# Mixture-of-experts kernel: an expert's transposes move into the next expert's first block, third products into the gate bank

## The chip, the cores and the metric

The kernel runs on one core of a Trainium2 chip. The metric is the device time of one execution in microseconds (us), as the median of several runs; lower is better. Beside it stands one execution taken with the hardware profiler, whose span (first to last instruction) is a little shorter than its device time.

## The reference, cut to what matters

The reference is two layers of a sequence mixer, a second hybrid mixer, and then a mixture of 16 experts over 256 tokens, of which each token takes two. The change touches only the last part:

```python
def _hier_moe(h, rg_w, rg_b, re_w, re_b, w_gate, w_up, w_down):
    hf = h.reshape(bsz * s, d)                       # 256 tokens x 1024
    ...                                              # combine: 256 x 16 weights, two per token not zero
    out = jnp.zeros((bsz * s, d), jnp.float32)
    for e in range(N_EXPERTS):                       # 16
        act = jax.nn.silu(hf @ w_gate[e]) * (hf @ w_up[e])                  # 256 x 512
        out = out + combine[:, e:e + 1] * (act @ w_down[e]).astype(jnp.float32)
    return out.astype(h.dtype).reshape(bsz, s, d)
```

All of it is float32.

## The kernel before, in words

The mixers fill the first 440 us. Then `experts` (L1934) takes the 16 experts in turn, four to a group (`q, j = divmod(e, 4)`). Weights come over one DMA queue (SyncE) in chunks of 2 MB, three per expert (two for gate and up, one for down), into a ring of seven buffers; `give_back` lets a buffer be filled again once the products that read it are done. All instructions of an engine run in the order in which the Python code writes them down (`manual_schedule`), so a step's place in the loop is its place in the queue of every engine that it uses.

For a group, `gather_all` picks the tokens of its four experts into `xg` with matmuls. An expert's tokens lie in slots: 32 in a first block, 32 in a second, 32 in a third. Numbers of tokens are read from memory on the chip, and `tc.If` runs the second block only above 32 tokens and the third only above 64. In this trace experts 0, 2, 4, 6, 8, 10 and 12 have a second block, 4 and 8 a third one as well, and 1, 3, 5, 7, 9, 11, 13, 14 and 15 the first alone (seen from the matmuls that ran). An `If` that is not taken still leaves a mark on its engines, which later instructions wait for as they would for the work itself.

The steps of an expert e, each with its engines:

- `gate_up(e)` (L1728, PE): the products with the gate and up weights. The first block goes to the PSUM bank `gu`, the other two to two banks of the pair `mbank("s")`; the bank holds gate and up, each as two partial sums (even steps in rows 0:64, odd ones in 64:128). `product32` (L1708) is eight steps k of two matmuls for a block, which show as 32 in the trace.
- `down(e - 1)` (L1799, PE): the product of the expert before with its down weights, into the bank `dn`.
- `activate(e)` (L1758, ScalarE and VectorE by turns): adds the partial sums, takes silu, multiplies, and leaves the result in `sg`; the second and third block within an `If`.
- `turn(e)` (L1784): four PE transposes of `sg` into an `mbank("s")` (L1789), copied by ScalarE to `aT` (L1791).
- `take(e - 1)` (L1806): copies the product in `dn` to `y`. Above 32 tokens that is a ScalarE copy (L1815) and a VectorE copy (L1816); else a ScalarE copy to `t3` (L1820) and two VectorE adds (L1797).
- `third(e - 1)` (L1825, PE) and `take_third(e - 1)` (L1834): the down product of a third block, in a bank of its own, and its copies to `y2` (L1837, L1797); without a third block a one-column matmul (`none`, L1726) and nothing.

After every second expert `split_all` or `split_third` (L1849, L1850) scales `y` and cuts it into a high and a low part on ScalarE and VectorE, and `scatter_all` (L1679, eight matmuls) adds the rows to the four accumulators. `spread` (L1636, L1637) transposes the pick matrix of a group for the scatters; its copies go over ScalarE. The order in the loop of before, on PE: `gate_up(e)`; for some e a scatter or a spread; `down(e - 1)`; `turn(e)`; `third(e - 1)`; for j = 1 the scatter of third blocks, for j = 3 the scatter of the first two experts and the next gather. ScalarE and VectorE run `activate(e)`, the copy of `turn(e)`, `take(e - 1)`, `take_third(e - 1)`, then the splits.

Of the kernel before, what the change touches and what calls it, by code (L numbers as in the profile page):

```python
# [19 lines left out]
NT, KT = T // P, D // P  # L20
# [10 lines left out]
N_EXP = 16  # L31
R1, R2 = 4, 5
WARM = (18, 12, 3, 4, 2)
# [213 lines left out]
class Net:  # L247
# [1457 lines left out]
        nc.gpsimd.memset(self.y[0], 0.0)  # L1705
        nc.gpsimd.memset(self.y2, 0.0)

    def product32(self, out, w, n, lhs):  # L1708


        for k in range(n):
            for i in range(2):
                r = 64 * (k % 2) + 32 * i
                self.nc.tensor.matmul(out[r:r + 32, :], lhs(k), w(k)[:, HALF * i:HALF * i + HALF], start=(k < 2),  # L1714
                                      stop=(k >= n - 2), tile_position=(0, r))
# [9 lines left out]

        self.nc.tensor.matmul(b[:, 0:1], self.zero, w.bitcast(BF16)[:, 1:2], start=True, stop=True)  # L1726

    def gate_up(self, e):  # L1728

        j, tc = e % 4, self.tc  # L1730
        ws, rs = zip(*[self.load() for _ in range(2)])
        ws = [a.rearrange("p (k n) -> p k n", k=4) for a in ws]

        def w(k):
            return ws[k // 4][:, k % 4, :]

        def x(s):
            return lambda k: self.S["xg"][:, k, s:s + 32]
        banks = self.gus = [self.gu, self.mbank("s"), self.mbank("s")]

        def none(i):
            for a in ws[2 - i:]:
                self.none(banks[i], a[:, 0, 0:1])
        if e + 1 < N_EXP:
            self.count(e + 1)
        self.product32(banks[0], w, KT, x(64 * j))
        with tc.If(self.n[e] > 32) as more:
            self.product32(banks[1], w, KT, x(64 * j + 32))
            with tc.If(self.n[e] > 64) as much:
                self.product32(banks[2], w, KT, x(256 + 32 * j))  # L1750
            with much.Else():
                none(2)
        with more.Else():
            none(1)
            none(2)
        self.give_back(*rs)
# [67 lines left out]

    def third(self, e, aT, wd):  # L1825

        b = self.mbank("s")
        with self.tc.If(self.n[e] > 64) as more:
            self.product32(b, lambda k: wd[:, k, :], 4, lambda k: aT[:, k, 64:96])
        with more.Else():  # L1830
            self.none(b, wd[:, 0, 0:1])
        return b
# [101 lines left out]
    def experts(self):  # L1934
        nc, m = self.nc, self.mw
        self.acc = [[self.ps.tile([P, HALF], F32, name=f"acc{t}{h}") for h in range(2)] for t in range(NT)]
        self.gu, self.dn = (self.ps.tile([P, HALF], F32, name=n) for n in ("gu", "dn"))
        self.clear(self.gu)
        self.clear(self.dn)
        for a in self.acc:  # L1940
            for b in a:
                self.open(b)
        self.sg = m.tile([P, HALF], F32, name="sg")
        nc.gpsimd.memset(self.sg, 0.0)
        S = self.S = {}
        self.wq = {}
        NQ = N_EXP // 4

        def gather_all():
            S["xg"] = m.tile([P, KT, 384], F32, name="xg")  # L1950
            for k in range(KT):
                self.gather(self.oh, S["xg"], k)
                if k == KT - 1:
                    self.wq[len(self.wq)] = self.weights(len(self.wq), self.oh)
        gather_all()
        self.residual()
        self.n, self.na = {}, {}
        self.count(0)
        aT = oT = None
        wd = lambda w: w.rearrange("p (k n) -> p k n", k=4)  # L1960
        E = mybir.EngineType
        nq = naq = None
        for e in range(N_EXP):
            q, j = divmod(e, 4)
            more, last = q + 1 < NQ, e == N_EXP - 1
            if last:
                w, r = self.load()
                self.down(e - 1, aT, wd(w))
                self.take(e - 1)
                self.scatter_all(oT[:, 0, :])  # L1970
                self.split_all(slice(0, 64), self.wq[q][:, 1:2])
            self.gate_up(e)
            if j == 0 and q:
                c = self.cnt[0:1, 16 + q:17 + q]
                nq = nc.values_load(c, engines=(E.PE,), min_val=0, max_val=T)
                naq = nc.values_load(c, engines=(E.Activation, E.DVE), min_val=0, max_val=T)
            if j == 1 and q:
                self.scatter_all(oT[:, 1, :])
            if j == 2 and q:
                oT = self.spread(self.oh)  # L1980
            if e and not last:
                w, r = self.load()
                self.down(e - 1, aT, wd(w))
            self.activate(e)
            if e == 0:
                oT = self.spread(self.oh)
            if last:
                self.tc.mark_branch_hint_location("further", "LikelyTaken")
                for _ in range(WARM[3]):
                    self.clear(self.dn)  # L1990
            a0, aT = aT, self.turn(e)
            if e and not last:
                self.take(e - 1)
                b = self.third(e - 1, a0, wd(w))
                self.give_back(r)
                self.take_third(e - 1, b, self.na[e - 1])
            if j == 1 and q:
                with self.tc.If(naq > 64):
                    self.split_third(q - 1, self.y[1:])
                with self.tc.If(nq > 64) as much:  # L2000
                    self.scatter_all(oT[:, 2, :])
                with much.Else():
                    for h in range(2):
                        for y in self.y[1:]:
                            self.nc.tensor.matmul(self.acc[1][h][:, 0:1], self.zero,
                                                  y.bitcast(BF16)[:, h * D + 1:h * D + 2], start=False, stop=False)
            if j == 2:
                if more:
                    self.oh = self.picks(q + 1)
                self.split_all(slice(0, P), self.wq[q][:, 0:1])  # L2010
            if j == 0 and q:
                self.split_all(slice(0, P), self.wq[q - 1][:, 1:2])
            if j == 3 and more:
                self.scatter_all(oT[:, 0, :])
                gather_all()
        i = self.free.pop()
        self.last = self.rings[i].tile([P, 4096], F32, name=f"wchunk{i}")
        for i in range(2):
            self.row(4 + i, self.last[:, i * D:(i + 1) * D], eng=nc.sync)
        free = list(self.free)[:4]  # L2020
        left = [(e - 1, a0, wd(w))]
        w, r = self.load()
        left.append((e, aT, wd(w)))
        for _ in range(WARM[4]):
            self.clear(self.dn)
        self.down(N_EXP - 1, aT, wd(w))
        self.take(N_EXP - 1, True)
        self.further(free, left, oT)
        self.scatter_all(oT[:, 1, :], last=True)
# [65 lines left out]
```

## Time and profile before

| what | value |
|---|---|
| median of 3 runs | 708.78 us (708.65 to 710.01) |
| the profiled execution's own time | 709.35 us |
| its span | 707.6 us |
| busy: PE, VectorE, ScalarE | 630.5, 445.2, 314.5 us |
| granted TensorE clock, mean of the span | 0.952 of full speed |

The profiled execution is 0.57 us above the median, and 1.75 us of it lie outside the span. The rows below give, of a timeline, the start in us from the start of the span, the length, engine, line, operation and tiles; in brackets stands how long the engine had been idle and what ended that. An engine named with a q (DVEq) is the engine's sequencer, which runs branches and marks. The granted clock is 1.00 at 2.4 GHz and 0.50 at 1.2 GHz.

### The profile page before, as it was taken

To read this page: it belongs to the slowest core of one execution; us is meant where nothing else is said; L and a number is where in the kernel's file an instruction comes from. 1 tells how busy PE (TensorE), PEld (TensorE's weight loads), DVE (VectorE), ACT (ScalarE), POOL (GpSimd) and SP (SyncE) were. 2 spreads that over 40 slices of the span, in tenths; PEclk is the share of its full clock that TensorE was granted. 3 is DMA by queue.
4 is the path that set the end of the run, shared out by engine and by line. 5 is a ranking of instruction groups with operands and counts; after the bars stand their busy time and mean duration, and the time that the engine had idled before them with its cause. 6 is when DMAs were issued, how large, how long until landed. Compare 5 with 4: busy or idle time off the path is not lost. (4 is left out here: it accounts for less than half of the span.)

```text
span 707.6 us, 11743 instructions
## 1 busy us (share of the span) xinstructions
PE 630.5 (89%) x4487; PEld 445.7 (63%) x4487; DVE 445.2 (63%) x1050; ACT 314.5 (44%) x618; POOL 7.2 (1%) x29
## 2 busy tenths in 40 slices
PE   7999999899899999999999979899786978797771
PEld 4789888688897887898888866326222623262221
DVE  5898677878986786886778867443314332434235
ACT  5764554557455544435545425333314232434230
POOL 1000000000000000000000000100000000000001
PEclk9999999999999999999989998999999989899786
DMA  8956313243560034735033389999999879889011
GB/s 319 424 172 240 120 82 119 90 177 133 223 230 13 5 120 181 322 138 204 35 119 120 120 338 396 389 422 426 427 425 427 380 320 396 359 356 353 7 63 61
DMA packets 15917, 163.65 MB, mean 231 GB/s; under 512 B 1888, under 2 KB 2144, under 8 KB 6624
## 3 DMA queue, kind: packets, MB, share of 16 engines
q1 hardware_dynamic: 15552, 161.84, 57.3%
q8 instruction: 48, 0.79, 0.4%
q10 hardware_dynamic: 288, 0.79, 0.3%
q14 instruction: 29, 0.24, 0.1%
HBM read 161.57 MB, written 1.05 MB: 230 GB/s over the span
## 5 line engine op out<-in xcount | busy, mean ns | idle before, releaser
L318 ACT ACTIVATE whi<-wchunk 128x1024 fp32r<-128x1024 f32 (+2 forms) x103 | 107.4, 1043 | 94.3 <-PE pj L420 49.1
L319 DVE TENSOR_TENSOR wlo<-wchunk,whi 128x1024 fp32r<-128x1024 f32 (+2 forms) x103 | 123.1, 1198 | 18.7 <-ACT whi L318 18.4
L419 PE MATMUL pj<-xh,whi 128*128 128x256 f32 (+1 forms) x440 | 126.8, 289 | 0.0
L420 PE MATMUL pj<-xl,whi 128*128 128x256 f32 (+1 forms) x440 | 126.3, 287 | 0.0
L421 PE MATMUL pj<-xh,wlo 128*128 128x256 f32 (+1 forms) x440 | 125.3, 285 | 0.0
L419 PEld LDWEIGHTS pj<-xh,whi 128*128 128x128 f32 (+1 forms) x440 | 82.6, 188 | 3.2 <-issue 2.2
L420 PEld LDWEIGHTS pj<-xl,whi 128*128 128x128 f32 (+1 forms) x440 | 82.7, 188 | 2.8 <-issue 1.9
L421 PEld LDWEIGHTS pj<-xh,wlo 128*128 128x128 f32 (+1 forms) x440 | 82.6, 188 | 1.8 <-issue 1.6
L1714 PE MATMUL gu<-wchunk,xg 128*32 128x512 f32 x512 | 69.6, 692 | 4.5 <-issue 3.5
L1767 DVE TENSOR_TENSOR tg<-tg,gu 64x256 f32<-64x256 f32 x32 | 13.2, 413 | 71.5 <-ACT tg L1766 71.4
L1714 PEld LDWEIGHTS gu<-wchunk,xg 128*32 128x32 f32 x512 | 17.8, 125 | 44.7 <-issue 43.5
L420 PE MATMUL pj<-wlo,xh 128*128 128x512 f32 (+2 forms) x112 | 40.4, 360 | 1.6 <-DVE wlo L319 1.6
L419 PE MATMUL pj<-whi,mh 128*128 128x512 f32 x96 | 38.4, 403 | 2.6 <-ACT mh L510 2.1
L420 PE MATMUL pj<-wlo,mh 128*128 128x512 f32 x96 | 38.1, 398 | 2.5 <-DVE wlo L319 2.5
L419 PE MATMUL pj<-whi,xh 128*128 128x512 f32 (+2 forms) x112 | 39.0, 354 | 1.1 <-ACT whi L318 1.1
L421 PE MATMUL pj<-whi,xl 128*128 128x512 f32 (+2 forms) x112 | 39.9, 356 | 0.0
L421 PE MATMUL pj<-whi,ml 128*128 128x512 f32 x96 | 37.5, 399 | 0.0
L1766 ACT ACTIVATE tg<-gu 64x256 f32<-64x256 f32 x32 | 12.2, 381 | 51.4 <-PE gu L1714 32.7
L553 ACT ACTIVATE prob<-bank,smst 128x128 f32<-128x128 f32 (+1 forms) x64 | 26.1, 419 | 18.4 <-DVE smst L551 18.4
L1679 PE MATMUL acc<-y,oT 128*128 128x512 f32 x80 | 25.0, 454 | 8.5 <-ACT y L1849 7.3
L1714 PE MATMUL mbs<-wchunk,xg 128*32 128x512 f32 x288 | 32.3, 592 | 0.0
L1789 PE MATMUL mbs<-cstm,sg 96*128 96x96 f32 x64 | 9.6, 278 | 20.0 <-DVEq L1774 9.4
(414 smaller groups left out, 1068.8 us busy)
## 6 DMA issues: line engine op xcount, KB each, us to landing
wchunk<-wstream SPq DMA_DIRECT2D x67, 2048.0 KB, 11.3
wchunk<-wstream SPq DMA_DIRECT2D x12, 512.0 KB, 10.7
wchunk<-wstream SPq DMA_DIRECT2D x2, 1536.0 KB, 9.7
wchunk<-wstream SPq DMA_DIRECT2D x2, 1024.0 KB, 8.4
wchunk<-wstream SPq DMA_DIRECT2D x4, 436.0 KB, 5.6
wchunk<-wstream SPq DMA_DIRECT2D x1, 1744.0 KB, 6.7
wchunk<-xt SPq DMA_DIRECT2D x4, 256.0 KB, 5.4
X<-x SPq DMA_DIRECT2D x4, 256.0 KB, 5.9
```

Source lines behind the costliest of these rows:

```text
L318: nc.scalar.activation(hi, w, AF.Copy)
L319: nc.vector.tensor_sub(lo, w, hi.bitcast(F32))
L419: mm(out, ah, bh, start=start, stop=False)
L420: mm(out, ah, bl, start=False, stop=False)
L421: mm(out, al, bh, start=False, stop=stop)
L553: nc.scalar.activation(p[:, e, j, :N], S[e][:, j, :], AF.Exp, bias=nm[:, e, j:j + 1], accum_out=sm[:, e, j:j + 1])
L1679: self.nc.tensor.matmul(self.acc[t][h], oT[r, t * P:(t + 1) * P], y[1 + i], start=False, stop=last and i == 1, **at)
L1714: self.nc.tensor.matmul(out[r:r + 32, :], lhs(k), w(k)[:, HALF * i:HALF * i + HALF], start=(k < 2), stop=(k >= n - 2), tile_position=(0, r))
L1766: nc.scalar.activation(tg[0:64, 0, s], b[64:128, s], AF.Copy)
L1767: V.tensor_add(tg[0:64, 0, s], tg[0:64, 0, s], b[0:64, s])
L1789: nc.tensor.transpose(ps[:, n * i:n * i + n], self.sg[p, P * i:P * i + P], self.ident[p, p])
```

## The change

`turn(e - 1)` is no longer called after `activate(e - 1)`. `gate_up(e)` gets it as `mid` and runs it ahead of the last two of the eight steps k of its first block; it asks for its two `mbank("s")` only after that. `take(e - 1)` thereby stands before the copy of `turn(e)` in the queues of ScalarE and VectorE. `third` writes to `self.gu` in place of a bank of its own. The scatter of third blocks moves from the end of an expert with j = 1 to after the gate and up products of the next one, ahead of `spread`; the scatter with `oT[:, 0, :]` moves from the end of j = 3 to after its gate and up products. The first `spread` comes before `activate(0)`. For the last expert, `turn(14)` and the scatter come first, then `down(14)`, and `turn(15)` stands after the loop.

```diff
--- before.py
+++ after.py
@@ -1705,10 +1705,12 @@
         nc.gpsimd.memset(self.y[0], 0.0)
         nc.gpsimd.memset(self.y2, 0.0)
 
-    def product32(self, out, w, n, lhs):
+    def product32(self, out, w, n, lhs, mid=None):
 
 
         for k in range(n):
+            if k == n - 2 and mid:
+                mid()
             for i in range(2):
                 r = 64 * (k % 2) + 32 * i
                 self.nc.tensor.matmul(out[r:r + 32, :], lhs(k), w(k)[:, HALF * i:HALF * i + HALF], start=(k < 2),
@@ -1725,7 +1727,7 @@
 
         self.nc.tensor.matmul(b[:, 0:1], self.zero, w.bitcast(BF16)[:, 1:2], start=True, stop=True)
 
-    def gate_up(self, e):
+    def gate_up(self, e, mid=None):
 
         j, tc = e % 4, self.tc
         ws, rs = zip(*[self.load() for _ in range(2)])
@@ -1736,14 +1738,19 @@
 
         def x(s):
             return lambda k: self.S["xg"][:, k, s:s + 32]
-        banks = self.gus = [self.gu, self.mbank("s"), self.mbank("s")]
+        banks = self.gus = [self.gu]
+
+        def before():
+            if mid:
+                mid()
+            banks.extend(self.mbank("s") for _ in range(2))
 
         def none(i):
             for a in ws[2 - i:]:
                 self.none(banks[i], a[:, 0, 0:1])
         if e + 1 < N_EXP:
             self.count(e + 1)
-        self.product32(banks[0], w, KT, x(64 * j))
+        self.product32(banks[0], w, KT, x(64 * j), before)
         with tc.If(self.n[e] > 32) as more:
             self.product32(banks[1], w, KT, x(64 * j + 32))
             with tc.If(self.n[e] > 64) as much:
@@ -1824,7 +1831,7 @@
 
     def third(self, e, aT, wd):
 
-        b = self.mbank("s")
+        b = self.gu
         with self.tc.If(self.n[e] > 64) as more:
             self.product32(b, lambda k: wd[:, k, :], 4, lambda k: aT[:, k, 64:96])
         with more.Else():
@@ -1964,12 +1971,18 @@
             q, j = divmod(e, 4)
             more, last = q + 1 < NQ, e == N_EXP - 1
             if last:
+                aT = self.turn(e - 1)
+                self.scatter_all(oT[:, 0, :])
                 w, r = self.load()
                 self.down(e - 1, aT, wd(w))
                 self.take(e - 1)
-                self.scatter_all(oT[:, 0, :])
                 self.split_all(slice(0, 64), self.wq[q][:, 1:2])
-            self.gate_up(e)
+                self.gate_up(e)
+            else:
+                def mid():
+                    nonlocal aT
+                    aT = self.turn(e - 1)
+                self.gate_up(e, mid if e else None)
             if j == 0 and q:
                 c = self.cnt[0:1, 16 + q:17 + q]
                 nq = nc.values_load(c, engines=(E.PE,), min_val=0, max_val=T)
@@ -1977,26 +1990,6 @@
             if j == 1 and q:
                 self.scatter_all(oT[:, 1, :])
             if j == 2 and q:
-                oT = self.spread(self.oh)
-            if e and not last:
-                w, r = self.load()
-                self.down(e - 1, aT, wd(w))
-            self.activate(e)
-            if e == 0:
-                oT = self.spread(self.oh)
-            if last:
-                self.tc.mark_branch_hint_location("further", "LikelyTaken")
-                for _ in range(WARM[3]):
-                    self.clear(self.dn)
-            a0, aT = aT, self.turn(e)
-            if e and not last:
-                self.take(e - 1)
-                b = self.third(e - 1, a0, wd(w))
-                self.give_back(r)
-                self.take_third(e - 1, b, self.na[e - 1])
-            if j == 1 and q:
-                with self.tc.If(naq > 64):
-                    self.split_third(q - 1, self.y[1:])
                 with self.tc.If(nq > 64) as much:
                     self.scatter_all(oT[:, 2, :])
                 with much.Else():
@@ -2004,6 +1997,23 @@
                         for y in self.y[1:]:
                             self.nc.tensor.matmul(self.acc[1][h][:, 0:1], self.zero,
                                                   y.bitcast(BF16)[:, h * D + 1:h * D + 2], start=False, stop=False)
+                oT = self.spread(self.oh)
+            if e == 0:
+                oT = self.spread(self.oh)
+            if j == 3 and more:
+                self.scatter_all(oT[:, 0, :])
+            if e and not last:
+                w, r = self.load()
+                self.down(e - 1, aT, wd(w))
+            self.activate(e)
+            if e and not last:
+                self.take(e - 1)
+                b = self.third(e - 1, aT, wd(w))
+                self.give_back(r)
+                self.take_third(e - 1, b, self.na[e - 1])
+            if j == 1 and q:
+                with self.tc.If(naq > 64):
+                    self.split_third(q - 1, self.y[1:])
             if j == 2:
                 if more:
                     self.oh = self.picks(q + 1)
@@ -2011,16 +2021,19 @@
             if j == 0 and q:
                 self.split_all(slice(0, P), self.wq[q - 1][:, 1:2])
             if j == 3 and more:
-                self.scatter_all(oT[:, 0, :])
                 gather_all()
+        self.tc.mark_branch_hint_location("further", "LikelyTaken")
+        for _ in range(WARM[3]):
+            self.clear(self.dn)
+        a0, aT = aT, self.turn(N_EXP - 1)
         i = self.free.pop()
         self.last = self.rings[i].tile([P, 4096], F32, name=f"wchunk{i}")
         for i in range(2):
             self.row(4 + i, self.last[:, i * D:(i + 1) * D], eng=nc.sync)
         free = list(self.free)[:4]
-        left = [(e - 1, a0, wd(w))]
+        left = [(N_EXP - 2, a0, wd(w))]
         w, r = self.load()
-        left.append((e, aT, wd(w)))
+        left.append((N_EXP - 1, aT, wd(w)))
         for _ in range(WARM[4]):
             self.clear(self.dn)
         self.down(N_EXP - 1, aT, wd(w))
```

## Rows read from the trace of the kernel before

**Rows 1.** Windows: busy time of PE, PEld, DVE, ACT, POOL, then PEclk, DMA share, GB/s.
```profile
450.00:500.00 50.00, 46.38 (x351) 21.01 (x355) 17.17 (x36) 16.75 (x34) 0.00 (x0) 0.97 1.00 420
...
600.00:650.00 50.00, 43.09 (x301) 19.87 (x293) 19.71 (x39) 18.36 (x36) 0.00 (x0) 0.93 0.87 347
```

**Rows 2.** Waits of the DMA queue from 420 us on: total us, times, longest.
```profile
SPq L292 <- PE mbs L1726: 128.2, 20, 15.2
```

**Rows 3.** Groups of instructions by line from 440 us on: busy, mean ns, idle before.
```profile
L1797 DVE TENSOR_TENSOR y<-tg,dn 32x512 f32<-32x512 f32 x18 | 12.2, 680 | 22.3 <-ACTq L1836 13.9 <-ACT tg L1820 8.1
...
L1789 PE MATMUL mbs<-cstm,sg 96*128 96x96 f32 x64 | 9.6, 278 | 20.0 <-DVEq L1774 9.4 <-DVE sg L1770 8.0 <-DVEq L1772 2.6
...
L1820 ACT ACTIVATE tg<-dn 64x512 f32<-64x512 f32 x9 | 5.3, 592 | 6.5 <-PE dn L1714 6.4
...
L1816 DVE COPY y<-dn 64x512 f32<-64x512 f32 x7 | 4.8, 692 | 24.0 <-ACTq L1836 14.8 <-ACT y L1815 9.2
...
L1815 ACT ACTIVATE y<-dn 64x512 f32<-64x512 f32 x7 | 4.0, 578 | 0.0
```

**Rows 4.** Line 1836, the branch of take_third: its marks, and who waited for it.
```profile
L1836 DVEq EVENT_SEMAPHORE  x12: 21/21/21, 463.7 to 670.6; - x12
...
  PEld dn L1714: 2.8, 1
```

**Rows 5.** Timeline of PE around the last expert.
```profile
667.44 0.52 PE L1789 MATMUL mbs<-cstm,sg 96*128 96x96 f32 x4 [0.83 <-DVEq L1772]
...
670.64 3.32 PE L1714 MATMUL dn<-wchunk,aT 128*32 128x512 f32 x16 [2.67 <-ACT y L1849]
673.89 2.12 PE L1679 MATMUL acc<-y,oT 128*128 128x512 f32 x8
675.93 3.64 PE L1714 MATMUL gu<-wchunk,xg 128*32 128x512 f32 x32
```

**Rows 6.** Timeline of PE after experts 2 (first row) and 4.
```profile
471.99 0.52 PE L1789 MATMUL mbs<-cstm,sg 96*128 96x96 f32 x4 [1.10 <-DVEq L1774]
...
505.72 0.52 PE L1789 MATMUL mbs<-cstm,sg 96*128 96x96 f32 x4 [3.98 <-DVE sg L1770]
...
506.91 4.98 PE L1714 MATMUL gu<-wchunk,xg 128*32 128x512 f32 x32 [0.57 <-issue]
```

**Rows 7.** Timeline of PE after expert 1.
```profile
457.75 3.65 PE L1721 MATMUL dn<-wchunk,aT 128*64 128x512 f32 x16
...
461.83 3.64 PE L1714 MATMUL gu<-wchunk,xg 128*32 128x512 f32 x32
```

**Rows 8.** Timeline of PE after expert 13.
```profile
646.85 3.65 PE L1721 MATMUL dn<-wchunk,aT 128*64 128x512 f32 x16
...
653.72 4.14 PE L1679 MATMUL acc<-y,oT 128*128 128x512 f32 x8 [2.73 <-ACT y L1849]
657.80 4.63 PE L1714 MATMUL gu<-wchunk,xg 128*32 128x512 f32 x32
```

**Rows 9.** Timeline of PE after experts 5 (first two rows) and 9.
```profile
518.00 1.92 PE L1714 MATMUL mbs<-wchunk,aT 128*32 128x512 f32 x16
...
522.91 5.34 PE L1714 MATMUL gu<-wchunk,xg 128*32 128x512 f32 x32 [0.47 <-issue]
...
592.63 0.49 PE L1679 MATMUL acc<-y,oT 128*128 128x512 f32 x1 [2.38 <-ACT y L1849]
...
595.23 3.64 PE L1714 MATMUL gu<-wchunk,xg 128*32 128x512 f32 x32
```

**Rows 10.** Timeline of PE after expert 0.
```profile
451.80 0.69 PE L1636 MATMUL dn<-cstm,oh 128*128 128x128 f32 x2 [2.46 <-ACT oT L1637]
...
453.06 4.60 PE L1714 MATMUL gu<-wchunk,xg 128*32 128x512 f32 x32
```

**Rows 11.** Windows of one us after two idle stretches; columns as in rows 1.
```profile
507.00:508.00 1.00, 1.00 (x8) 0.31 (x12) 0.58 (x1) 0.38 (x1) 0.00 (x0) 0.50 1.08 459
...
593.00:594.00 1.00, 0.71 (x4) 0.49 (x4) 1.00 (x2) 0.27 (x1) 0.00 (x0) 1.00 1.00 426
```

## The prediction

> **What bounds the kernel now.** I first asked the windows who is short of what in the expert part. PE is busy 46.4 of 50 us at 450 to 500 and 43.1 at 600 to 650, while the DMA share falls from 1.00 to 0.87 [rows 1]. The DMA queue's own waits say why: it stands 128.2 us in 20 waits for PE to hand buffers back [rows 2]. So the weights are ahead, and PE's sequence with its waits sets the end. What PE waits for stands in the groups: the transposes (L1789) are busy 9.6 us and are preceded by 20.0 us of idle PE, ended by VectorE's activation [rows 3]. The timeline shows the pattern: after expert 4 PE idles 3.98 us, transposes in 0.52 us, and starts the next first block 1.19 us after the transposes began, at 506.91 [rows 6]. Idle PE costs twice: that block takes 4.98 us in place of 3.64 [rows 6, 7], since the granted clock stands at 0.50, the 1.2 GHz level, after the idle stretch [rows 11].
>
> **The idea and what it meets.** The change puts products ahead of the transposes: `down`, and three quarters of the next first block. If nothing else held that block, the 20.0 us would mostly go. But `third` now writes the gate bank, and `take_third` reads it, so the next first block may start only when ScalarE and VectorE have gone past the branch of `take_third(e - 1)`. They get there after `activate(e)` and `take(e - 1)`, which stand ahead of it in their queues. That the branch is mostly not taken doesn't help: it leaves 12 marks, and PE waited 2.8 us for one of them, that of expert 13, which has no third block [rows 4]. There VectorE's mark came at 670.6 and PE's `down` began at 670.64 [rows 4, 5]. So the block that was to cover the activation waits for the activation and for the copies too.
>
> The Trainium skill bears on this (PSUM — Partial Sum Buffer, section "PSUM bank collisions raise a hardware error"): two engines must not touch one bank and quadrant at once, and accesses are to be ordered by bank, not address. By that rule the wait is needed and the time is my sum; without it, it is the first rival's.
>
> **The turn from one expert to the next, part by part.** S is the start of the transposes now, G that of the next first block.
>
> *Even experts 2 to 12 (six turns).* At S the activation is done. What follows on VectorE is two adds of 0.680 us [rows 3]; the ScalarE copy ahead of them, 0.592 us [rows 3], runs beside the last activation product. Two branches lie on the way; no row gives their whole price. The mark itself is 21 ns [rows 4]; I take 0.2 us each, with ends 0 and 0.4. New G is S + 1.36 + 0.4 = S + 1.8, against S + 1.19 [rows 6]: 0.6 later. Then the block holds the transposes, 0.52 [rows 6], without a wait of their own. 1.1 slower each, 6.6 in all.
>
> *Extra in turns 6 and 10.* A scatter now goes before `spread`, and ScalarE's copies of `spread` go before `activate`, so the activation starts later by all of it. After 10 that is eight matmuls, 2.12 us [rows 5]: +2.0. After 6 it is four one-column matmuls and a branch: +0.5, estimated.
>
> *Turn 1.* `down(0)` ends at 457.75 + 3.65 = 461.40. Its two copies run one after the other, 0.578 and 0.692 [rows 3], with about 0.35 for semaphores and branches: new G is 463.0 against 461.83 [rows 7]. With the transposes +1.7.
>
> *Turn 13.* The same copies after 646.85 + 3.65 = 650.50 give 652.15 against 657.80, where the wait for the split of third blocks (2.73) and a slow scatter (4.14) went before [rows 8]. That is -5.65, the transposes +0.5, and the block of 4.63 us returns to 3.64: -1.0. Together -6.1.
>
> *Turns 5 and 9.* The third block of 4 and 8 is there, so its copy is awaited in earnest. After 5 the product ends at 519.92, now 0.5 earlier without the transposes; copy, adds and branch take 0.6 + 1.4 + 0.4: G is 521.8 against 522.91 [rows 9], with the transposes in the block -0.6. After 9 the product ended at 592.63 - 2.38 = 590.25; the same gives 592.1 against 595.23 [rows 9], with the transposes -2.6.
>
> *Turn 0.* PE idles 2.46 us in `spread`, since ScalarE copies it behind the activation, and the next block takes 4.60 [rows 10]. With `spread` ahead, the activation starts later by its copies and the transposes inside the block wait about 1.2: +0.5.
>
> *Turns 3, 7, 11.* The gather lies between, longer than the copies: only the order changes, 0.
>
> *The end.* After 14 the scatter of 2.12 delays S from 667.44 to 669.5. The copies take 1.8, the first split another 0.8, so the scatter for 12 and 13 runs from 672.0; its last quarter waits for the second split, to 674.2. `down(14)` at full clock is half of its 3.32 and a little, 1.9, and G is 676.3 against 675.93 [rows 5]: +0.4.
>
> Moves that cost nothing are `give_back` and the weight queue (the weights are ahead by the DMA share; if that cover went, a 2 MB chunk late would be next) and the copies of `turn`, which ScalarE makes while PE runs the block's last quarter.
>
> Sum: 6.6 + 0.5 + 2.0 + 1.7 - 6.1 - 0.6 - 2.6 + 0.5 + 0.4 = +2.4.
>
> *The clock.* After experts 2 and 12 PE's idle stretch grows from 1.10 us [rows 6] to some 2.9 in one piece. Of two such stretches before, 2.46 was followed by a block of 4.60 and 2.38 by one of 3.64 [rows 9, 10, 11]. A fall costs 1.0 on the block and 0.3 on transposes; at one half each for two turns I add 1.3. Ends: 0, or 6 if they both fall and the longer idle after 4, 6, 8, 10 (some 5.6 in place of 4.0 after 4) costs 0.8 more each.
>
> The total is +3.7, from 709.35 to 713.05 in the profiled execution. That ran 0.57 above the median, so 712.5 as a median.
>
> **The rivals.**
>
> *A, the block doesn't wait (faster).* If the marks come early, or nothing ties the block to them, PE fills the 20.0 us before the transposes [rows 3] and keeps the 2.73 and 2.38 of rows 8 and 9. Where the activation is long (4, 6, 8, 10), block and `down` cover some 5 us, and 1 to 2 stay: -6. With about 4 of clock back, -21 to -24: near 688. It decides at the first matmul of a block after `third`: if it starts within 0.6 us of it at expert 4, A holds. Against it stands the 2.8 us wait of [rows 4]. Chance 0.10.
>
> *B, the branches are cheap and the clock is kinder (same or a little faster).* With branches at 0.05 us, ten turns give 3 back; with no fall after 2 and 12 it is 1.3 less, and if the block after 5 (5.34 [rows 9]) runs at full clock, 1.7 less. All three: 709.35 + 3.7 - 6.0 = 707, as a median 706.5; any one: 709.2 to 711.2, so this case covers 705 to 710. For it: the idle after 5 becomes one stretch of 2.4, near the stretch of 2.38 that cost nothing. Against it: all the longer stretches do get longer. Chance 0.24, half of it within 0.2%.
>
> *C, the moves don't do what they say.* The transposes do stand in the block, but wait for nothing: the wait is now ahead of the block. That is the forecast itself.
>
> **How the numbers follow.** The forecast of a slower kernel has 0.66, B 0.24, A 0.10. A difference of 0.2% (1.4 us) is about what a measurement of this kernel can tell from none. Slower by more than that is the forecast alone, 0.66; within it half of B, 0.12; faster the other half and A, 0.22. The range takes in B from below and, above, the sum with the dear end of the clock: 712.5 + 4.7 and 2 for dearer branches, 719. From 705 to 719 leaves out A and the tails, some 0.2.
>
> **What would show it.** In the changed profile the idle time before L1789 should be near zero but for the turn after 0, and in its place the first matmul of a `gu` block should show some 2 to 5.5 us of idle, ended by VectorE's L1836 or L1797: about 5 us after expert 4, 2.9 after 2 and 12, 1.5 after 1 and 13. The scatter after 13 should be gone from there, with its 2.73, and the time from expert 13's last product to the next block should be 5.6 shorter. The turn after 10 should be 2.6 longer. If the blocks start right after `third`, the forecast is wrong; if they wait, but the clock rows show fewer low stretches than before, the size is.

## The result and the profile after

The changed kernel is slower. On the same chip it takes 717.25 us (median of 4 runs, 715.70 to 718.62) against 708.89 us (4 runs, 708.65 to 710.01): a ratio of 1.0114, 95% interval 1.0089 to 1.0139, or +8.4 us where +3.7 was forecast. A second set on another chip, shown below as `after_again`, gives 715.86 against 710.22, 1.0075 (1.0048 to 1.0102), +5.6 us. The profiled execution, the slowest of the four, took 718.62 us with a span of 716.8 (709.35 and 707.6 before); its mean granted clock is 0.947 (0.952).

The windows of after, columns as in [rows 1]:

```profile
450.00:500.00 50.00, 42.59 (x281) 18.03 (x277) 17.62 (x36) 17.07 (x34) 0.00 (x0) 0.90 0.99 409
600.00:650.00 50.00, 41.03 (x289) 18.26 (x287) 17.41 (x34) 16.28 (x31) 0.00 (x0) 0.97 0.86 356
```

PE is busy 42.6 and 41.0 us in stretches where it was busy 46.4 and 43.1 [rows 1]. The groups by line of after, from 440 us on, say where it stands idle:

```profile
L1716 PE MATMUL gu<-wchunk,xg 128*32 128x512 f32 x512 | 75.7, 721 | 38.0 <-ACT y L1856 27.1 <-issue 4.6 <-ACTq L1843 3.1
...
L1796 PE MATMUL mbs<-cstm,sg 96*128 96x96 f32 x64 | 9.1, 266 | 2.5 <-DVEq L1779 2.5
```

The first blocks of before, in the same view:

```profile
L1714 PE MATMUL gu<-wchunk,xg 128*32 128x512 f32 x512 | 69.6, 692 | 4.5 <-issue 3.5 <-DVE wq L1652 1.0
```

The 20.0 us ahead of the transposes [rows 3] are down to 2.5; 38.0 us now stand ahead of the first blocks, where it was 4.5. The timeline of PE, ScalarE and VectorE after expert 4 shows one of those waits:

```profile
508.73 1.90 PE L1716 MATMUL dn<-wchunk,aT 128*32 128x512 f32 x16
...
510.56 0.18 PE L1728 MATMUL gu<-wchunk,zero 128*128 128x1 bf16 x1
...
513.78 0.59 ACT L1827 ACTIVATE tg<-dn 64x512 f32<-64x512 f32 x1
513.79 0.68 DVE L1777 TENSOR_TENSOR sg<-tg 32x512 f32<-32x512 f32 x1 [0.69 <-ACT tg L1776]
514.54 1.39 DVE L1804 TENSOR_TENSOR y<-tg,dn 32x512 f32<-32x512 f32 x2
...
516.09 1.94 PE L1716 MATMUL gu<-wchunk,xg 128*32 128x512 f32 x8 [5.35 <-ACT y L1856]
```

`third(4 - 1)` is a one-column matmul into the gate bank at 510.56, since expert 3 has no third block. The next first block starts at 516.09, after the last activation product (L1777) and the two adds of `take` (L1804, 1.39 us). The profile names line 1856, the split that starts 0.78 us earlier; but no operand of the block hangs on the split. What ends there is VectorE's way past the branch of `take_third`, right behind the adds. The line of that branch, asked from 515 to 517 us and then as a whole, shows the mark and, for the turns after 1 and 13, in which the profile names the branch itself, PE's wait for it:

```profile
L1843 DVEq EVENT_SEMAPHORE  x1: 21/21/21, 516.0 to 516.0; - x1
...
L1843 DVEq EVENT_SEMAPHORE  x12: 21/21/21, 466.4 to 680.9; - x12
...
  PE gu L1716: 3.1, 2
```

The adds end at 515.93, VectorE's mark comes at 515.97, and the block starts at 516.09. In all eight turns with a mark ahead of the block (after 1, 2, 4, 6, 8, 10, 12 and 13) the block starts 0.12 us behind it.

The clock falls in these waits. Timeline rows of three first blocks of after (24 of 32 matmuls each, 2.78 us at full speed), and windows of one us in two of them:

```profile
454.08 5.35 PE L1716 MATMUL gu<-wchunk,xg 128*32 128x512 f32 x24 [2.19 <-DVE tg L1774]
...
466.50 2.78 PE L1716 MATMUL gu<-wchunk,xg 128*32 128x512 f32 x24 [1.54 <-ACTq L1843]
...
532.72 2.78 PE L1716 MATMUL gu<-wchunk,xg 128*32 128x512 f32 x24 [2.30 <-issue]
```

```profile
455.00:456.00 1.00, 1.00 (x12) 0.33 (x8) 0.35 (x1) 0.59 (x1) 0.00 (x0) 0.50 1.03 442
...
533.00:534.00 1.00, 1.00 (x12) 0.31 (x8) 0.00 (x0) 0.00 (x0) 0.00 (x0) 1.00 1.06 442
```

After turn 0 (2.19 us idle) the block runs at 0.50, the 1.2 GHz level; after expert 5 (2.30 us idle) at 1.00. The blocks are slow too behind the 2.86 us after experts 2 and 12 (the 24 matmuls take 4.29 and 4.11 us) and the 5.3 to 5.4 us after 4, 6, 8 and 10 (4.40 to 5.35 us).

### The profile page after: what moved, and what is told of

It reads as the page before. It is cut to its first block, busy times and chain, and to the rows that moved or that the text cites. A ratio compares the mean times of both kernels' runs of the same rounds, so it can differ in the third digit from the quotient of the medians.

```text
span 716.8 us, 11754 instructions
## 1 busy us (share of the span) xinstructions
PE 634.8 (89%) x4487; PEld 444.0 (62%) x4487; DVE 445.2 (62%) x1050; ACT 315.1 (44%) x618; POOL 7.2 (1%) x29
## 5 line engine op out<-in xcount | busy, mean ns | idle before, releaser
L1716 PE MATMUL gu<-wchunk,xg 128*32 128x512 f32 x512 | 75.7, 721 | 38.0 <-ACT y L1856 27.1
L1798 ACT ACTIVATE aT<-mbs 128x384 f32<-128x384 f32 x16 | 7.8, 490 | 58.9 <-PE mbs L1796 58.9
L1723 PE MATMUL dn<-wchunk,aT 128*64 128x512 f32 x112 | 25.6, 598 | 0.0
```

The source lines that it names most:

```text
L1723: self.nc.tensor.matmul(out[64 * i:64 * i + 64, :], lhs(k), w(k)[:, HALF * i:HALF * i + HALF], start=(k == 0), stop=(k == n - 1), tile_pos ...
L1798: nc.scalar.activation(aT.rearrange("p a n -> p (a n)"), ps[:, 0:4 * n], AF.Copy)
```

## The experiments

### Is it the bank that holds the first block?

`no_tie` computes and copies a third product only for experts 4 and 8, the only ones with a third block here. `third_own_bank` is the changed kernel with one line back as it was; `before_gate_bank` the kernel before with that line alone.

```diff
 no_tie, in the loop of after
-                b = self.third(e - 1, aT, wd(w))
+                if e - 1 in (4, 8):
+                    b = self.third(e - 1, aT, wd(w))
...
-                self.take_third(e - 1, b, self.na[e - 1])
+                if e - 1 in (4, 8):
+                    self.take_third(e - 1, b, self.na[e - 1])
 third_own_bank, third() of after
-        b = self.gu
+        b = self.mbank("s")
 before_gate_bank, third() of before
-        b = self.mbank("s")
+        b = self.gu
```

> The changed kernel without third and its copy, branches included, for every expert but 4 and 8 (the only ones with a third block here, so no work is lost). Theory, the gate bank ties the first block to the copies: the idle PE before gu blocks (38.0 us in all in the changed kernel) falls to the 2.3 us each after 5 and 9 and the gather's, the block starts within 0.7 us of down, and what is left of the activation shows as 0.5 to 1 us before the transposes inside the block after 4, 6, 8, 10; the time falls by 23 and some 5 of clock, to 686 to 696. Rival, the activation and copy chain or the weights bound the part anyway: the wait reappears elsewhere and the time stays above 705.

> The kernel before with one part of the change alone: third writes the gate bank. Theory: the next first block then waits for the mark of take_third, which there stands behind the copy of the transposes too; as at the end of the kernel before, S + 3.2 in place of S + 1.2 after 2, 4, 6, 8, 10, 12 and 2 more after 1: +14, with the clock up to +19, 721 to 728. Rival, the bank doesn't matter: 708 to 711.

> The changed kernel with one part undone: third in a bank of the pair again, at its new place. Its first matmul then waits for the activation of the second block, but the next gate block no longer for the copies. Theory: idle before gu blocks becomes S + 0.6 in place of S + 1.6 after the six even experts, and 0.6 after down for 1 and 13, after third for 5 and 9: -12, with clock -2 more, 702 to 706. Rival, the copies are not on the path: 715 to 718.

All against the kernel before on the same chip (711.14 us, 13 runs): `no_tie` 691.82 us, ratio 0.9726 (0.9688 to 0.9763), as expected; `before_gate_bank` 730.69, 1.0261 (1.0227 to 1.0294), more than the 721 to 728 expected; `third_own_bank` 685.36, 0.9637 (0.9587 to 0.9686). The turn after expert 4, timelines of PE in the three, in this order:

```profile
503.27 1.90 PE L1716 MATMUL dn<-wchunk,aT 128*32 128x512 f32 x16
504.99 1.47 PE L1716 MATMUL gu<-wchunk,xg 128*32 128x512 f32 x12
```

```profile
512.40 0.52 PE L1789 MATMUL mbs<-cstm,sg 96*128 96x96 f32 x4 [3.99 <-DVE sg L1770]
512.76 0.17 PE L1726 MATMUL gu<-wchunk,zero 128*128 128x1 bf16 x1
515.65 4.91 PE L1714 MATMUL gu<-wchunk,xg 128*32 128x512 f32 x24 [2.72 <-ACT y L1849]
```

```profile
503.85 1.90 PE L1716 MATMUL dn<-wchunk,aT 128*32 128x512 f32 x16
505.68 0.18 PE L1728 MATMUL mbs<-wchunk,zero 128*128 128x1 bf16 x1
506.39 1.06 PE L1716 MATMUL gu<-wchunk,xg 128*32 128x512 f32 x8 [0.53 <-issue]
```

Without the tie the block starts as soon as `down` is through. With the bank alone, in the old order, PE pays both the 3.99 us ahead of the transposes, as in [rows 6], and 2.72 us ahead of the block. With the new order and the third product in its own bank it pays 0.53. So the bank is the cause, shown from both sides: put into the kernel before it costs 19.6 us, low clock included; taken out of the changed one it gives some 32 (717.25 - 685.36, from two chips). From the first block of 0 to that of 15 the profiles give 234.3 us before, 243.8 in the changed kernel, 210.7 in `no_tie` and 209.9 in `third_own_bank`. So the two ways of cutting the tie are worth the same, and the 6 us by which their medians differ lie mostly ahead of this stretch and behind it. That also leaves out the rival that the one line helps by changing the turns of the `mbank("s")` pair: in `no_tie` the pair is taken in turn as in the changed kernel.

The Trainium skill (PSUM — Partial Sum Buffer, "PSUM bank collisions raise a hardware error") has accesses guarded by bank and quadrant, not by address. Here the writers and the reader share the rows as well as the bank, so no run tells one kind of order from the other; what is measured is what keeping them in order costs.

`third_own_bank` missed its expectation by 17 us on the good side. I had taken the third product's own bank, which is one that the second block's sums have to be read from first, for a long wait. It is one only after experts 6 and 10, of which the first (timeline of PE in `third_own_bank`):

```profile
533.97 0.16 PE L1728 MATMUL mbs<-wchunk,zero 128*128 128x1 bf16 x1 [2.27 <-DVE tg L1774]
534.71 0.83 PE L1716 MATMUL gu<-wchunk,xg 128*32 128x512 f32 x4 [0.57 <-issue]
```

What it waits for is the reading of the sums, not the chain of silu, products and copies behind it.

### How much of it is the clock?

Matmuls of zeros into an open accumulator (a sum in PSUM that the scatters are still adding to) change nothing in it and keep PE busy in a wait. `keep_busy` has ten of them in six waits of the changed kernel, `before_keep_busy` ten in four waits of the kernel before; `after_kept_busy` and `before_kept_busy` fill all the long waits of the two, and `after_again` is the changed kernel itself beside them.

```diff
+    def idle(self, n):
+        for _ in range(n):
+            self.nc.tensor.matmul(self.acc[0][0].rearrange("p (a n) -> p a n", a=4), self.zero,
+                                  self.zero[:, None, :].to_broadcast([P, 4, P]), start=False, stop=False)
...
 keep_busy, ahead of take_third
+                if j in (0, 2) and e < 14:
+                    self.idle(10)
 before_keep_busy, ahead of turn(e)
+            if e in (4, 6, 8, 10):
+                self.idle(10)
 after_kept_busy, ahead of take_third; and 6 after the first spread
+                self.idle({1: 4, 2: 9, 4: 18, 5: 7, 6: 18, 8: 18, 9: 7, 10: 18, 12: 9, 13: 4}.get(e, 0))
 before_kept_busy, ahead of turn(e); and 7 ahead of the first spread, 4, 7, 9 ahead of the scatter for j = 1
+            self.idle({2: 2, 4: 14, 6: 13, 8: 14, 10: 14, 12: 2}.get(e, 0))
```

> The changed kernel with ten matmuls of zeros, added to an accumulator, after third of the experts 1, 3, 5, 7, 9, 11 (2.1 us at full clock, inside waits of 2.9 to 5.4 us). Theory on the clock: of the time that PE loses at 0.50 after these waits (16 us by the lengths of the blocks) most goes, and the waits stay as they are: -8 to -12, 705 to 709. Rival, the low clock hides in waits anyway, or the zeros delay the products: 715 to 720.

> The kernel before, with ten matmuls of zeros into an open accumulator (2.2 us at full clock, they add nothing to the sums) ahead of the transposes after experts 4, 6, 8 and 10, where PE idles some 4 us before them. It prices the clock in the kernel before: the first blocks after these four take 4.98, 5.22, 6.3 and 5.7 in place of 3.64 us. If the fall of the clock is set by these idle stretches, most of those 7 to 8 us come back: 5 to 8 us under the kernel before, and the four blocks near 3.64. The rival: the clock falls for other reasons (the power of the stretch as a whole), then the blocks stay as long and the time is within 1.5 us of before.

> The changed kernel with matmuls of zeros into an open accumulator in every wait ahead of a first block (18 after experts 4, 6, 8, 10, 9 after 2 and 12, 7 after 5 and 9, 4 after 1 and 13, 6 after the spread of expert 0; 10 of them take 2.2 us), fewer than the wait is long, so that the order and the end of each wait stay. It shows the change with the clock taken out, beside the same of the kernel before. My theory: the waits are as the forecast had them and cost 7 to 9 us at full clock (its own sum, 2.4 us with the 4.5 us of low clock that it counted as gone, is 6.9; the three turns with a gather give 2 more), so this run stands 6 to 10 us above before_kept_busy, and at 700 to 705 us. The rival: the loss is the clock's in the main, and the two kernels are within 4 us of each other with the clock kept up.

> The kernel before with matmuls of zeros in the waits that end late there: 7 ahead of the spread of expert 0, 2, 13 or 14 ahead of the transposes after the even experts, 4, 7 and 9 ahead of the scatter after 5, 9 and 13. The first blocks should all be near 3.64 us. My theory: it comes to 695 to 700 us, 6 to 10 us under after_kept_busy. The rival: 700 us or more, within 4 us of after_kept_busy.

> The changed kernel once more, on the chip of the two kernels with zeros, to set all four times side by side: 716 to 718 us, 7 to 9 above the kernel before.

`keep_busy`: 708.58 us (10 runs), ratio 0.9956 (0.9930 to 0.9982) to before, where the changed kernel has 1.0114; by the medians 8.7 less, in the expected range. Its blocks after 2 and 12 are back at 2.78 us for 24 matmuls; those after 4, 6, 8 and 10, with 3.1 to 3.2 us of the wait left idle, still take 4.1 to 4.5. `before_keep_busy`: 706.00 (7 runs) against 710.33, ratio 0.9921 (0.9887 to 0.9956): 4.3 less, a little short of the 5 to 8 expected; the blocks after 4, 6 and 10 came back to 3.64 us, and so did the one after 5, but the one after 8 took 5.08 us all the same, and the one after 12, where no zeros stand, some 5.3. Its executions lie anywhere from 698.76 to 708.26 us. The last three ran on one chip beside before at 710.22 (14 runs): `after_kept_busy` 704.46, ratio 0.9918 (0.9889 to 0.9946); `before_kept_busy` 697.22, 0.9802 (0.9774 to 0.9830); `after_again` 715.86, a little less than expected. Windows of `after_kept_busy` and of `before_kept_busy`:

```profile
500.00:550.00 50.00, 45.24 (x327) 16.61 (x321) 17.71 (x33) 16.03 (x31) 0.00 (x0) 1.00 1.00 420
550.00:600.00 50.00, 47.77 (x345) 20.12 (x342) 16.05 (x28) 14.95 (x27) 0.00 (x0) 1.00 0.88 367
```

```profile
500.00:550.00 50.00, 44.35 (x311) 18.50 (x304) 19.08 (x35) 17.69 (x35) 0.00 (x0) 1.00 1.01 426
550.00:600.00 50.00, 46.23 (x341) 19.44 (x341) 16.22 (x30) 15.48 (x30) 0.00 (x0) 1.00 0.98 407
```

The clock is at 1.00 in both, and every first block takes its full-speed time; in the expert part low clock remains only from the end of expert 14 on. With the clock kept up the change costs 704.46 - 697.22 = 7.2 us; with the clock as granted, 5.6 on that chip. The zeros took 11.4 us off the changed kernel and 13.0 off the kernel before. The rival of `after_kept_busy`, that the loss is the clock's in the main, falls: it is the waits'. What the change does to the clock, 5.6 - 7.2 = -1.6 us, is small beside the 2 to 6 us by which executions of one kernel differ.

### The moved scatter, and the turns with a gather

`scatter_back` puts the scatter of third blocks back at the end of j = 1; `turn_before_gather` the transposes of 3, 7 and 11 back ahead of the gather.

```diff
 scatter_back
             if j == 2 and q:
-                with self.tc.If(nq > 64) as much:
-                    self.scatter_all(oT[:, 2, :])
...
                 with self.tc.If(naq > 64):
                     self.split_third(q - 1, self.y[1:])
+                with self.tc.If(nq > 64) as much:
+                    self.scatter_all(oT[:, 2, :])
...
 turn_before_gather
-                self.gate_up(e, mid if e else None)
+                self.gate_up(e, mid if e and j else None)
...
             self.activate(e)
+            a0 = aT
+            if j == 3 and more:
+                aT = self.turn(e)
...
-                b = self.third(e - 1, aT, wd(w))
+                b = self.third(e - 1, a0, wd(w))
```

> The changed kernel with one part undone: the scatter of the third blocks is back at the end of an expert with j = 1 (5, 9, 13). My theory, from the steps for turns 5, 6, 9, 10, 13 and 14: the scatter takes as many matmuls wherever it stands, but back there it waits again for the split (2.73 us after 13, some 2.4 after 9) and runs at the low clock after 13 (4.14 in place of 2.12), while after 10 and 14 2.1 us go away again; so +2.4 + 2.0 (9) - 2.1 (10) + 4.9 to 6.9 (13) - 2.1 (14): 3 to 8 us slower than the changed kernel, 720 to 725. The rival: the wait for the copies takes all of it up (the block waits for take_third anyhow, and the split runs right behind it), so that the place of the scatter makes no difference above 1.5 us: 716 to 719.

> The changed kernel with the transposes of experts 3, 7 and 11 back ahead of the gather that follows them, as before; all other turns as changed. The forecast had those three turns at 0; the trace of the changed kernel gives +0.65 us each at full clock, which I put down to the transposes (0.5 us inside the next first block, where they cover nothing) and to copies that queue behind the gather's. By that theory turning them back gives some 2 us: 714 to 716, with the three intervals from first block to first block 0.5 to 1 us shorter. The rival: the wait for the activation comes back ahead of the transposes and eats it: 717 to 719.

`scatter_back`, whose timeline of PE after expert 13 stands below: 719.58 us, ratio 1.0126 (1.0110 to 1.0142). By the median that is 2.3 over the changed kernel, between what theory and rival gave, and its interval overlaps that of the changed kernel (1.0114). The trace is clearer. From first block to first block the intervals of experts 9 and 13 are 3.1 and 3.6 us longer than in the changed kernel, those of 10 and 14 are 0.9 and 3.4 shorter. My price for 13 (4.9 to 6.9) forgot that PE waits there in the changed kernel too: 2.34 us ahead of the scatter take the place of 1.55 ahead of the block, and the rest of the 3.6 is about the scatter itself, now at full speed:

```profile
670.97 0.50 PE L1679 MATMUL acc<-y,oT 128*128 128x512 f32 x1 [2.34 <-ACT y L1856]
671.76 1.89 PE L1679 MATMUL acc<-y,oT 128*128 128x512 f32 x7 [0.28 <-DVE y L1857]
```

`turn_before_gather`: 715.60 us (6 runs), ratio 1.0088 (1.0061 to 1.0116). The median lies where the theory had it, but that doesn't settle it, since the interval overlaps that of the changed kernel. The trace speaks for the rival, with another wait than the one that it named. The intervals of 4, 8 and 12 lose the 0.6 us of the transposes, but those of 3, 7 and 11 don't get shorter: that of 3 is 17.76 us with its first blocks at full speed, against 17.00 in `after_kept_busy`, since the gather, which writes the gate bank too, now waits for `take_third` (timeline of PE in `turn_before_gather`):

```profile
489.02 0.59 PE L1661 MATMUL gu<-oh,xnh 128*128 128x384 f32 x2 [0.45 <-DVEq L1843]
```

The median is low for another reason, at least in the profiled execution: the clock. Up to the gather after expert 3 this kernel is the changed one, and its waits after 0 and 2 are the same, but no block fell behind them. First the two blocks here, then the one after 2 in the changed kernel, whose block after 0 stands above:

```profile
453.22 2.78 PE L1716 MATMUL gu<-wchunk,xg 128*32 128x512 f32 x24 [2.19 <-DVE tg L1774]
...
476.60 2.78 PE L1716 MATMUL gu<-wchunk,xg 128*32 128x512 f32 x24 [2.86 <-ACT y L1856]
```

```profile
479.15 4.29 PE L1716 MATMUL gu<-wchunk,xg 128*32 128x512 f32 x24 [2.86 <-ACT y L1856]
```

The block after 12, again behind 2.86 us, takes 2.78 us here too, and 4.11 in the changed kernel.

A part of what made these turns longer was another move, and the two kept-busy traces show it at full clock. After expert 3 in `after_kept_busy`, then in `before_kept_busy`:

```profile
482.28 3.65 PE L1723 MATMUL dn<-wchunk,aT 128*64 128x512 f32 x16
485.87 0.18 PE L1734 MATMUL gu<-wchunk,zero 128*128 128x1 bf16 x1
485.90 0.61 PE L1661 MATMUL mbs<-oh,xnh 128*128 128x384 f32 x2
...
492.98 0.64 PE L1716 MATMUL gu<-wchunk,xg 128*32 128x512 f32 x4
```

```profile
481.31 2.09 PE L1679 MATMUL acc<-y,oT 128*128 128x512 f32 x8
483.23 0.51 PE L1661 MATMUL mbs<-oh,xnh 128*128 128x384 f32 x2
...
489.91 0.64 PE L1714 MATMUL gu<-wchunk,xg 128*32 128x512 f32 x4
```

Before, the scatter stood between `down` and the gather and covered the copies of `take`; now the gather follows `down` at once, its copies queue behind those of `take`, and it takes 492.98 - 485.90 = 7.1 us in place of 6.7. That is 0.4 of the 0.66 us; the rest is about what the transposes cost more inside a block (4.26 - 3.64 = 0.62 us) than behind `down` (0.39).

### Versions that beat both kernels

`own_bank_spread_later` is `third_own_bank` with the first spread one expert later. `own_bank_tuned` adds to it the scatter back in front of the gather and zeros ahead of the third product after 6 and 10.

```diff
 both, against third_own_bank
-            if e == 0:
+            if e == 1:
                 oT = self.spread(self.oh)
 own_bank_tuned
-            if j == 3 and more:
-                self.scatter_all(oT[:, 0, :])
...
+                self.idle({6: 8, 10: 8}.get(e, 0))
                 b = self.third(e - 1, aT, wd(w))
...
             if j == 3 and more:
+                self.scatter_all(oT[:, 0, :])
                 gather_all()
```

> The faster version found so far (the changed kernel with the third block in a bank of its own, 685.4 us) with the first spread one expert later, behind the first blocks of expert 1 in place of those of expert 0, so that its copies no longer stand ahead of the activation of expert 0 (there the next first block waits 2.2 us for the gate sums to be read). Expected 2 us less: 682 to 684.5. The rival: the DMA share is already 1.00 from 430 to 600 us, so that the time is the weights' and stays at 684.5 to 686.5.

> The version of own_bank_spread_later (683.5 us) with two more edits that the traces call for: the scatter of experts 3, 7 and 11 back between take_third and the gather, where it covers the copies of take (behind down the gather follows at once, and its interval is 0.66 us longer in all three turns), and eight matmuls of zeros ahead of the third product after experts 6 and 10, which waits 2.3 us there and is followed by first blocks of 4.2 to 4.3 us in place of 2.8. By my theory -3 x 0.4 to 0.66 and -2 x 1.4 of clock: 679 to 681.5 us. The rival: nothing of the kind is left on the path, the weights set the time: 683 to 685 us.

`own_bank_spread_later`: 683.53 us (4 runs), ratio 0.9630 (0.9614 to 0.9646). The step is in the expected direction, but its interval overlaps that of `third_own_bank`. `own_bank_tuned`: 677.53 us (6 runs; before 709.09), ratio 0.9536 (0.9507 to 0.9565), better than expected. The intervals of 7 and 11 are 16.58 us each; in `third_own_bank` that of 11, with its block at full speed too, is 17.71. So the scatter as a cover is worth 1.1 us in these two turns, more than the 0.66 at most that I gave it. After 3 it gives only 0.2 (17.47 against 17.69), since the third product waits 0.71 us there. The groups of `own_bank_tuned` from 440 us on:

```profile
L1716 PE MATMUL gu<-wchunk,xg 128*32 128x512 f32 x512 | 61.1, 597 | 3.9 <-issue 3.0 <-DVE wq L1652 0.9
...
L1802 PE MATMUL mbs<-cstm,sg 96*128 96x96 f32 x64 | 8.7, 258 | 3.2 <-DVEq L1785 1.8 <-DVE sg L1783 1.1 <-DVEq L1787 0.3
```

3.9 us of idle time are left ahead of the first blocks (38.0 in the changed kernel), 3.2 ahead of the transposes (20.0 before).

## Why the prediction was right in direction and short in size

**Right: the mechanism, and the waits.** The forecast had some 5.6 us of idle PE after expert 4, 2.9 after 2 and 12, 1.5 after 1 and 13; the trace has 5.35, 2.86 and 1.54 to 1.55. It had the wait for the split after 13 gone, which it is: the time from expert 13's last product to the next block is 5.63 us shorter, where 5.65 was forecast. Rival A was right about the worth of the moved transposes (it said near 688 without the tie; `no_tie` gives 691.8) and wrong that nothing ties the block.

The row that the forecast had for the tie shows less than it was taken for. In [rows 4] PE's `down(14)` waited 2.8 us up to the mark, but it writes `dn`, which the adds of `take(13)` read until 670.53, 0.05 us ahead of the mark (timeline of before):

```profile
669.14 1.39 DVE L1797 TENSOR_TENSOR y<-tg,dn 32x512 f32<-32x512 f32 x2 [1.90 <-ACTq L1836]
```

It would have waited about as long without a branch. That a branch which is not taken holds the next first block is shown by `no_tie` and `before_gate_bank`, not by that row. In rival B, "any one" should begin at 712.5 - 3.0 = 709.5, not 709.2; nothing hangs on it.

To set the steps against measurements, the times from one first block to the next of `after_kept_busy` less those of `before_kept_busy` are free of the clock in all turns but that of 14. There `down(14)` takes 3.24 us before (1.92 at full speed) and seven matmuls of the scatter take 3.35 after (1.89), 1.3 and 1.5 us too long, which nearly cancel. The forecast is put on the same footing: the transposes of an expert count in the interval after it, and the 4.4 us of slow matmuls that it took as gone (the block after 13, 1.0; the scatter there, 2.0; `down(14)`, 1.4) are taken out of the steps and counted with the clock.

| interval from the first block of | forecast at full clock | measured |
|---|---|---|
| 0 and 1 | 0.5 + 1.2 = 1.7 | 2.9 |
| 2, 4, 8, 12 | 0.5 + 0.6 = 1.1 each | 1.3, 1.0, 0.9, 1.3 |
| 6, 10 | 1.6, 3.1 | 1.5, 3.2 |
| 3, 7, 11 | 0 each | 0.66, 0.64, 0.66 |
| 5, 9 | -0.6, -2.6 | -0.6, -2.5 |
| 13 | -5.65 + 2.0 + 0.5 = -3.1 | -3.6 |
| 14 | 0.5 + 0.4 + 1.4 = 2.3 | 1.8 |
| sum | 6.8 | 9.2 |

**Failed: the clock.** The forecast counted 4.4 us of slow time as gone and added 1.3 for new falls: -3.1 in all. In the profiled executions the first block of 15 comes 9.48 us later, counted from that of 0, with the clock as granted, and 9.17 with it kept up. The clock's share of the change is +0.3 there, and -1.6 by the medians of the one chip, in place of -3.1. The step that failed is "at one half each for two turns I add 1.3". The matmuls counted as gone do run at full speed in the trace, but new falls took the time again. The falls after 2 and 12 came both and cost 1.5 and 1.3 us on the block, and falls elsewhere had been left at no cost: turn 0's block takes 5.35 us for its first 24 matmuls, 2.6 too long, where it lost 1.0 before; and the scatter after 14 takes 3.35 us for seven matmuls, 1.5 too long, as much as `down(14)` gave back. How many of these falls come is in part chance: in the profile of `turn_before_gather` the same three waits after 0, 2 and 12 are followed by none. So the 3.4 us between forecast and trace are the size of this term in one execution.

**Failed: turns 3, 7 and 11, "The gather lies between, longer than the copies: only the order changes, 0".** It gave 0.66 each, 2.0 in all. I had costed the scatter in its new place, but not as the cover that it was for the copies of `take` (0.4 of the 0.66), nor the dearer place of the transposes (most of the rest).

**Smaller: turn 0.** It was 0.5 in the forecast and is some 1.3 at full clock: the interval of 0 is 0.4 shorter (11.02 against 11.42 us), and the block after it, with the transposes in it, 1.7 longer (5.34 against 3.64 in the kept-busy traces). The transposes inside that block wait 1.04 us, near the 1.2 of the forecast. What the forecast doesn't name is the wait ahead of the block, 2.19 us, until `activate(0)`, now behind the copies of `spread`, has read the sums out of the bank that the block is to write; in `own_bank_spread_later`, with `spread` out of the way, the block doesn't wait and the interval is 7.14 us. In the table the two intervals come to 2.9, since the zeros in `before_kept_busy` shorten its interval of 0 by 0.3, to 11.09 us.

The two failed steps are 3.4 and 2.0 us; together with the small ones they make the 5.8 that part 9.48 from 3.7. The profiled span grew by 9.2. Ahead of the experts it is 1.43 longer, which isn't the change's: in the profile of `after_again` the first block starts at 441.60 us, before at 441.64. Behind the first block of 15 it is 1.71 shorter, where `down(15)` takes 1.92 us in place of 3.48; the forecast stops at that block and has no term for it.

## What to carry to other kernels

Before work is moved in front of a wait, list the PSUM banks that it writes and who reads them: a bank shared with a rarely taken branch makes its writer wait for that branch's place in the readers' queues, not for the branch's own length. Give the rare product a bank that its readers leave early. And when a step is moved away, ask what it covered in its old place, and price the clock of every wait that gets longer, not of the new ones alone, and as a range: the same waits were followed by a fall in one execution and by none in another.

## What the runs showed of the hardware

A product of one column (0.18 us) in the gate bank cost 19.6 us in a kernel whose PE was idle 20.0 us ahead of the transposes already; after expert 4 it pays 3.99 and 2.72 us one behind the other. Matmuls of zeros in PE's waits, some 27 and 20 us of them, took 11.4 us off the changed kernel and 13.0 off the kernel before, with every first block back at its full-speed time. And the length of an idle stretch alone doesn't tell whether the clock falls: in the changed kernel 2.19 us after expert 0 were followed by a block at 0.50 and 2.30 us after 5 by one at 1.00; in `turn_before_gather`, with the same waits of 2.19 us after 0 and 2.86 us after 2, both blocks ran at full speed. What else decides it was not tried.
